# Products that add on in their own banks: three edits around two seven-product stages, key heads in pairs, and small cuts at two norms

## The chip, the cores and the metric

One core of one Trainium2 chip runs the whole program. A core has TensorE (PE in the profile; PEld is its weight load), VectorE (DVE), ScalarE (ACT), GpSimd (POOL), SyncE (SP, which here issues transfers) and 16 DMA engines. Matmul results land in PSUM, eight banks of 128 partitions by 512 fp32 values; everything else is in SBUF. The metric is the device time of one execution in microseconds, as the median of three runs; one execution is also profiled.

## The reference

A two-layer backbone over 256 latent tokens and 256 context tokens, width 1024. Every sub-layer is modulated by a conditioning vector (shift, scale, gate from `ada_w`) and followed by a residual norm:

```python
for i in range(DEPTH):                       # DEPTH = 2
    ml = _modulation(c, ada_w[i], ada_b[i]); mc = _modulation(c_ctx[None, :], ada_w[i], ada_b[i])
    hl = _modulate(x, ml[0], ml[1]); hc = _modulate(xc, mc[0], mc[1])
    # layer 0: mLSTM mixer; layer 1: multi-head latent attention (MLA), 8 heads
    x = _layer_norm(ALPHA * x + ml[2] * yl, ln_g[i, 0], ln_b[i, 0])
    f = _conv_ffn(_modulate(x, ml[3], ml[4]), ffn_w_in[i], ffn_conv_w[i], ffn_conv_b[i], ffn_w_out[i])
    x = _layer_norm(ALPHA * x + ml[5] * f, ln_g[i, 1], ln_b[i, 1])
    # the same for the context tokens xc, in layer 0 only
```

In the mLSTM, `v = x_m @ w_v` (2048 by 2048). In the feed-forward part, `(silu(conv(gate)) * up) @ w_out` (2816 by 1024). In MLA, context and latent tokens give a compressed row `ckv` (256) and a rotary key (64) through `w_dkv`, a norm, and keys and values of the heads through `w_ukv`; queries go through `w_dq` (384) and two further matrices.

## The kernel before, in words

**Precision.** Every fp32 operand is split in two parts, hi (rounded) and lo (the rest), and every product is three matmuls that add up in one bank: hi·hi, hi·lo, lo·hi (`mm3`, L381–L385). A split of a tile is one ScalarE copy for hi and one VectorE subtraction for lo (`split`, L387–L389).

**Weights.** `Stream` (L235–L352) reads the weights in one fixed order: a transfer into a raw tile, a ScalarE copy for hi (L323), a VectorE subtraction for lo (L326). Three split tiles are alive at a time (tile w), further ones are made as early ones are used up, up to eight ahead; some tiles of later use have a wide pool of their own (wu). Loads are issued by SyncE (L281).

**Order.** The program is traced through a scheduler which places each instruction in its engine's queue by dependencies and its own estimate of time, with `keep_in_program_order` (`pin`) for those that must stay where they are written. Background work, such as norms, is a generator that gives up control at each `yield`; `tick(n)` runs n steps of it between matmul groups and `drain` finishes it. `self.ps` takes the next of eight banks in a ring and waits until its last reader is done.

**The two seven-product stages.** `w_v` (L787–L849, banks named tok) computes a 2 by 2 block product with seven block products in place of eight, as sums of operands (S1 to S4) and of results. The results p6, p1, p7, p5 (two banks each, so all eight) come first. ScalarE copies p1 out of its banks, VectorE adds p6 to the copy (u2, later u4), p7 to that (u3), and forms p5 − u3 and p5 − u4; the last three products (weights v21, vt4, v22) then run into three fresh pairs of banks, and VectorE adds them to p1's copy, u3 and u4. It does so twice (two column halves). `w_fout0` (L1365–L1500, banks named y) does the same for the first layer's second feed-forward matrix, in the weight order yt2, y11, yt3, yt1 (six rounds), then y21, y22, yt4 (six each). There each result is also multiplied by the gate (L1454, L1464), added to the scaled residual row (L1455, L1465), and its norm statistics taken (L1457, L1466). `residual()` does this for p1's copy, u4, u3 and the finished fourth block while y21 and y22 run; `add()` does it for the last three products. The context half is normalised (L1507–L1514), transposed (tile zT, L1199), modulated (zm, L1206 and L1208) and split (hc, L1211 and L1212) while yt4 runs; the latent half (hl) follows under the key heads.

**Layer 1's front.** `mla_ctx` makes the context's dkv rows, their norm and transposes (`dkv_T`, L1572–L1581, tile ckT). `ukn(g)` (L1583) makes the keys of eight heads, two in a bank, each head split right after its own matmuls; `uv` (L1598) the values. Then follow `ln_T` of the latent half (L1192), dkv on hl, dq (eight steps over k), `dkv_T` for the latent rows, `ukn(1)` and the queries. `ln_x` (L1218) multiplies the rows by ln_g and ln_b (tiles gr and br, L1227 and L1228) for a later residual.

**Norms.** `ln_rows` (L1131–L1174) normalises a 128-row tile in two halves, VectorE on the first 512 columns (L1172) and ScalarE on the rest (L1173). Where the caller gives the second row tile three banks (`fine`), the first row tile is normalised by ScalarE alone (L1170). `ffn_in` (L1292) of the last layer, with `both`, has for its first pair of tiles (p = 0) a plain mm3 of 256 columns; for the others one matmul of 512 columns covers hi·hi and hi·lo side by side and a second of 256 adds lo·hi, and a copy and an add join the halves. `ada_split` (L454–L460) splits the conditioning matrix's tiles (adas) ahead of the first matmuls (adar, L474).

Of the kernel before, what the change touches and what calls it, by code (L numbers as in the profile page):

```python
# [354 lines left out]
class K:  # L355
# [25 lines left out]
    def mm3(self, out, w, x, start, stop):  # L381
        mm = self.nc.tensor.matmul
        mm(out, w[0], x[0], start=start, stop=False)  # L383
        mm(out, w[0], x[1], start=False, stop=False)  # L384
        mm(out, w[1], x[0], start=False, stop=stop)  # L385
# [68 lines left out]
    def ada_split(self, g):  # L454
        r = []
        for w in self.adaw.pop(g):
            hi, lo = [self.pool.tile([128, 1024], F32R, tag="u", name="adas", bufs=NU) for _ in range(2)]
            self.split(hi, lo, w)
            r.append((hi, lo))
        return r  # L460
# [326 lines left out]
    def w_v(self):  # L787


        nc, st, A = self.nc, self.st, self.xA  # L790
        self.vd = self.dr.tile([H0, 4, 128, 512], F32, name="vd")

        def prod(ps, a, w, h, j):
            for b in range(2):
                ts = slice(b * 128, (b + 1) * 128)
                cs = slice(h * 512, (h + 1) * 512)
                self.mm3(ps[b], (a[:, 0, ts], a[:, 1, ts]), (w[0][:, cs], w[1][:, cs]), j == 0, j == 7)
# [6 lines left out]
        for p in range(2):  # L804
# [9 lines left out]
            u1, u3, u4 = [], [], []  # L814
            for b in range(2):
                u = self.s2("u1")
                nc.scalar.copy(u, p1[b])
                u1.append(u)
                u = self.s2("u2")
                nc.vector.tensor_tensor(u, p6[b], u1[b], op=ALU.add)  # L820
                u4.append(u)
            for b in range(2):
                u = self.s2("u3")
                nc.vector.tensor_tensor(u, p7[b], u4[b], op=ALU.add)
                u3.append(u)
# [14 lines left out]
            for b in range(2):  # L840
                nc.vector.tensor_tensor(u1[b], p2[b], u1[b], op=ALU.add)
                put(2 * p, b, u1[b])
            for b in range(2):
                nc.vector.tensor_tensor(u3[b], p4[b], u3[b], op=ALU.add)
                put(2 * p, 2 + b, u3[b])
            for b in range(2):
                nc.vector.tensor_tensor(u4[b], p3[b], u4[b], op=ALU.add)
                put(2 * p + 1, b, u4[b])
# [282 lines left out]
    def ln_rows(self, pss, xres, gate, fin=None):  # L1131
# [3 lines left out]
        for t in range(2):  # L1135
# [33 lines left out]
            if fine and t == 0:  # L1169
                nc.scalar.activation(z[:, 0:512], z[:, 0:512], AF.Identity, bias=nm, scale=rs)  # L1170
            else:
                nc.vector.tensor_scalar(z[:, 0:512], z[:, 0:512], mv[:, 0:1], rs, op0=ALU.subtract, op1=ALU.mult)  # L1172
            nc.scalar.activation(z[:, 512:1024], z[:, 512:1024], AF.Identity, bias=nm, scale=rs)  # L1173
# [118 lines left out]
    def ffn_in(self, l, hT, n, nt, pre=(), both=None):  # L1292
# [6 lines left out]
        for p in range(NF):  # L1299
            pss = []  # L1300
            for j in range(2):
# [5 lines left out]
                else:  # L1307
# [13 lines left out]
                    if both is not None and p > 0:  # L1321
# [43 lines left out]
    def w_fout0(self, x1d, mid):  # L1365
# [25 lines left out]
        def prod(ps, x, w, i, bs=(0, 1)):  # L1391
            for h in range(2 if i < 5 else 1):
                j = 2 * i + h
                a = A[x, j]
                for b in bs:
                    ts = slice(b * 128, (b + 1) * 128)
                    cs = slice(h * 512, (h + 1) * 512)
                    self.mm3(ps[b], (a[:, 0, ts], a[:, 1, ts]), (w[0][:, cs], w[1][:, cs]), j == 0, j == 10)
# [6 lines left out]
        n = 0  # L1405
        for i in range(6):
            for name, ps, x in (("yt2", p6, "S2"), ("y11", p1, "1"), ("yt3", p7, "S3"), ("yt1", p5, "S1")):
# [21 lines left out]
                n += 1  # L1429
        stats = [self.tiny(12, "st").rearrange("p (a b) -> p a b", b=6) for _ in range(4)]  # L1430
        u1, u3, u4, vv = [], [], [], []
        for b in range(2):
            u = self.s2("u1")
            nc.scalar.copy(u, p1[b])
            u1.append(u)
            u = self.s2("u2")
            nc.vector.tensor_tensor(u, p6[b], u1[b], op=ALU.add)
            u4.append(u)
        for b in range(2):
            u = self.s2("u3")  # L1440
            nc.vector.tensor_tensor(u, p7[b], u4[b], op=ALU.add)
            u3.append(u)
        for b in range(2):
            v = self.s2("v")
            nc.vector.tensor_tensor(v, p5[b], u3[b], op=ALU.subtract)
            nc.vector.tensor_tensor(u4[b], p5[b], u4[b], op=ALU.subtract)
            vv.append(v)

        def residual():

            for us, g, c in ((u1, 0, lo), (u4, 0, hi), (u3, 1, lo), (vv, 1, hi)):
                for b in range(2):
# [7 lines left out]
        def add(g, c, ps):  # L1460
            for b in range(2):
# [522 lines left out]
```

## Time and profile before

| what | value |
|---|---|
| median of 3 runs | 1387.09 us (1386.12 to 1387.57) |
| the profiled execution | 1386.22 us |
| its span, first to last instruction | 1384.1 us |
| outside the span | 2.1 us |
| busy: TensorE, VectorE, ScalarE | 1354.0, 1090.0, 713.1 us |
| mean granted TensorE clock | 0.996 |

The stages named in the text lie here on the time line of the profiled execution: start-up to about 62 us, `w_v` from 207 to 360, `w_fout0` from about 930 to 1044, layer 1's front from there to about 1115, the norm behind the attention output at 1184 to 1190, and the last feed-forward stage to the end. A group's row gives line, engine, operation, tiles as output and inputs, shape and type, a count, and then total busy time and the mean in ns; behind a bar stands the engine's idle time ahead of the group with what ended it. A row of the time line starts with the start and the length in us. A row of waits names the waiting engine and tile, the releasing one, and the total, the count and the longest.

### The profile page before, as it was taken

What the parts mean: (1) busy time and instruction counts of PE and PEld (TensorE: products, weight loads), DVE (VectorE), ACT (ScalarE), POOL (GpSimd) and SP (SyncE); (2) the same over time, 40 slices, a digit from 0 to 9 for tenths busy, and PEclk for the clock granted to TensorE, in tenths of its full rate; (3) what the DMA queues carried; (4) which work ended last, traced back from release to release, by engine and by line L of the source; (5) the groups of instructions that cost most, each with busy time, mean ns of one, the idle gap of its engine ahead of it and who ended that gap; (6) DMA issues with size and microseconds to landing.
All of it is one profiled execution on the core that took longest, in us unless ns stands there. A gap on an engine that the chain in (4) does not pass through costs nothing.

```text
span 1384.1 us, 18592 instructions
## 1 busy us (share of the span) xinstructions
PE 1354.0 (98%) x6567; PEld 1123.2 (81%) x6567; DVE 1090.0 (79%) x1768; ACT 713.1 (52%) x1221; POOL 121.6 (9%) x215
## 2 busy tenths in 40 slices
PE   7999999999999999999999999999999999999997
PEld 3788888888788888878898888888777888888886
DVE  6598857687688697779799878668898789788873
ACT  6585534435444555364643434334637567466660
POOL 0033000011011011120002000000001001000100
PEclk9999999999999999999999999999999999999999
DMA  9689847789666364766747877646987425256750
GB/s 338 227 293 316 290 156 247 239 286 302 214 200 204 105 232 132 250 193 228 241 147 239 300 230 234 212 145 229 312 231 226 137 99 202 109 185 185 252 202 31
DMA packets 97900, 297.58 MB, mean 215 GB/s; under 512 B 12136, under 2 KB 24808, under 8 KB 97808
## 3 DMA queue, kind: packets, MB, share of 16 engines
q1 hardware_dynamic: 68672, 218.52, 47.5%
q0 software_dynamic: 17472, 57.57, 13.3%
q10 hardware_dynamic: 11664, 20.32, 4.1%
q8 instruction: 51, 0.84, 0.2%
q14 instruction: 41, 0.34, 0.1%
HBM read 262.90 MB, written 33.46 MB: 214 GB/s over the span
## 4 chain that ended last, share of the span: by engine, by line
PE 91%; DVE 5%; ACT 2%; issue 1%; DMA 0%; SPq 0%; DVEq 0%; ACTq 0%
PE fin L1320 9%; PE fin L383 6%; PE fin L384 6%; PE fin L385 6%; PE tok L383 6%; PE tok L384 6%; PE tok L385 6%; PE y L384 5%; PE y L385 5%; PE y L383 5%; PE qk L383 4%; PE qk L385 4%; PE qk L384 4%; PE up L383 2%; PE up L385 2%; PE up L384 2%
## 5 line engine op out<-in xcount | busy, mean ns | idle before, releaser
L326 DVE TENSOR_TENSOR w<-raw,w 128x1024 fp32r<-128x1024 f32 (+3 forms) x290 | 348.1, 1203 | 141.3 <-ACT w L323 140.3
L323 ACT CAST w<-raw 128x1024 fp32r<-128x1024 f32 (+3 forms) x290 | 300.4, 1037 | 306.2 <-PE tok L385 88.6
L512 DVE SCALAR_TENSOR_TENSOR junk<-ar,bc 128x1024 f32<-128x1024 f32 x128 | 156.0, 1218 | 4.9 <-ACT bc L554 2.1
L384 PE MATMUL fin<-h,w 128*128 128x512 f32 (+1 forms) x376 | 141.2, 376 | 0.0
L385 PE MATMUL fin<-h,w 128*128 128x512 f32 (+1 forms) x376 | 140.9, 375 | 0.0
L383 PE MATMUL fin<-h,w 128*128 128x512 f32 (+1 forms) x376 | 140.8, 376 | 0.1
L1320 PE MATMUL fin<-h,w 128*128 128x256 f32 (+1 forms) x640 | 113.0, 339 | 0.0
L1320 PEld LDWEIGHTS fin<-h,w 128*128 128x128 f32 x640 | 98.2, 189 | 14.7
L383 PE MATMUL qk<-xc,w 128*128 128x512 f32 x256 | 100.7, 393 | 0.0
L385 PE MATMUL qk<-xc,w 128*128 128x512 f32 x256 | 99.9, 390 | 0.0
L384 PE MATMUL qk<-xc,w 128*128 128x512 f32 x256 | 99.8, 390 | 0.0
L384 PEld LDWEIGHTS fin<-h,w 128*128 128x128 f32 x376 | 70.8, 188 | 12.9 <-DVE h L1212 0.2
L385 PEld LDWEIGHTS fin<-h,w 128*128 128x128 f32 x376 | 70.8, 188 | 12.9
L383 PEld LDWEIGHTS fin<-h,w 128*128 128x128 f32 x376 | 70.5, 188 | 13.1 <-ACT h L1211 0.3
L383 PEld LDWEIGHTS qk<-xc,w 128*128 128x128 f32 x256 | 48.1, 188 | 10.0 <-issue 0.4
L385 PEld LDWEIGHTS qk<-xc,w 128*128 128x128 f32 x256 | 48.1, 188 | 9.9
L384 PEld LDWEIGHTS qk<-xc,w 128*128 128x128 f32 x256 | 48.1, 188 | 9.7
L383 PE MATMUL up<-hT,w 128*128 128x512 f32 x128 | 50.5, 394 | 0.5 <-ACT hT L388 0.5
L384 PE MATMUL up<-hT,w 128*128 128x512 f32 x128 | 50.1, 392 | 0.5 <-DVE hT L389 0.5
L385 PE MATMUL up<-hT,w 128*128 128x512 f32 x128 | 50.1, 391 | 0.3 <-DVE w L389 0.3
L383 PE MATMUL tok<-w,hT 128*128 128x512 f32 x128 | 49.8, 389 | 0.0
L384 PE MATMUL tok<-w,hT 128*128 128x512 f32 x128 | 49.8, 389 | 0.0
(463 smaller groups left out, 3151.2 us busy)
## 6 DMA issues: line engine op xcount, KB each, us to landing
raw<-in_ws SPq DMA_DIRECT2D x287, 512.0 KB, 4.3
ar<-in_adaT SPq DMA_DIRECT2D x80, 512.0 KB, 4.6
adaw<-in_ada_w SPq DMA_DIRECT2D x32, 256.0 KB, 6.7
t2d<-raw ACTq DMA_DIRECT2D x13, 512.0 KB, 4.9
raw<-t2d SPq DMA_DIRECT2D x13, 512.0 KB, 6.3
raw<-in_ws POOLq DMA_DIRECT2D x13, 512.0 KB, 8.0
zr<-fd ACTq DMA_DIRECT2D x33, 128.0 KB, 3.9
xmd<-xr POOLq DMA_DIRECT2D x16, 256.0 KB, 5.0
```

Source lines behind the costliest of these rows:

```text
L323: k.nc.scalar.copy(h[:, :cols], src)
L326: k.nc.vector.tensor_sub(l[:, :cols], src, h[:, :cols])
L383: mm(out, w[0], x[0], start=start, stop=False)
L384: mm(out, w[0], x[1], start=False, stop=False)
L385: mm(out, w[1], x[0], start=False, stop=stop)
L512: nc.vector.scalar_tensor_tensor(o, w, 1.0, self.bc[j], op0=ALU.mult, op1=ALU.mult, accum_out=col[:, k, j:j + 1])
L1320: nc.tensor.matmul(o, a, b, start=k == 0 and i == 0, stop=k == 7 and i == 1)
```

## The change

Six edits. (1) `mm3` gets `on`: with it the first matmul adds to what is in the bank. In both seven-product stages u2 = p6 + p1's copy, as before, but p7 + u2 and p5 − u2 are written back into the banks of p7 and p5, and the last three products add on in the banks of p1, p7 and p5. In `w_v` ScalarE then copies the six finished banks out. In `w_fout0` the copies of p1 are pinned right behind p1's last product, `residual()` is gone, `add` scales the residual itself, and `last` does the fourth block. (2) The last tile of `ada_split(0)` is split in two halves. (3) `ln_rows` with `fine`, second row tile: VectorE takes columns 0–255 and 256–767, ScalarE the last 256. (4) `ffn_in` with `both`: p = 1 also runs as mm3 of 256 columns. (5) `ukn` splits a pair of heads after the second head. (6) `dkv_T(rows, 2)` runs behind the seventh step of dq.

```diff
-    def mm3(self, out, w, x, start, stop):
+    def mm3(self, out, w, x, start, stop, on=False):
...
-        mm(out, w[0], x[0], start=start, stop=False)
+        mm(out, w[0], x[0], start=start, stop=False, skip_group_check=on)
...
     def ada_split(self, g):
+            n = 512 if g == 0 and w is ws[-1] else 1024
+            for i in range(0, 1024, n):
+                self.split(hi[:, i:i + n], lo[:, i:i + n], w[:, i:i + n])
...
     def w_v(self):
-            u1, u3, u4 = [], [], []
+            u2 = []
             for b in range(2):
                 u = self.s2("u1")
                 nc.scalar.copy(u, p1[b])
-                nc.vector.tensor_tensor(u, p6[b], u1[b], op=ALU.add)
-            for b in range(2):
-                nc.vector.tensor_tensor(u, p7[b], u4[b], op=ALU.add)
+                u2.append(u)
+            for b in range(2):
+                nc.vector.tensor_tensor(u2[b], p6[b], u2[b], op=ALU.add)
+            for b in range(2):
+                nc.vector.tensor_tensor(p7[b], p7[b], u2[b], op=ALU.add)
             for b in range(2):
                 v = self.s2("v")
-                nc.vector.tensor_tensor(v, p5[b], u3[b], op=ALU.subtract)
-                nc.vector.tensor_tensor(u4[b], p5[b], u4[b], op=ALU.subtract)
+                nc.scalar.copy(v, p7[b])
+                nc.vector.tensor_tensor(v, p5[b], v, op=ALU.subtract)
+                nc.vector.tensor_tensor(p5[b], p5[b], u2[b], op=ALU.subtract)
                 put(2 * p + 1, 2 + b, v)
-            p2, p4, p3 = pair("tok"), pair("tok"), pair("tok")
             for i in range(4):
-                for name, ps, x in (("v21", p2, 2), ("vt4", p4, 3), ("v22", p3, "S4")):
+                for name, ps, x in (("v21", p1, 2), ("vt4", p7, 3), ("v22", p5, "S4")):
...
-                        prod(ps, A[x, 2 * i + h], w, h, 2 * i + h)
+                        prod(ps, A[x, 2 * i + h], w, h, 2 * i + h, True)
...
-            for b in range(2):
-                nc.vector.tensor_tensor(u1[b], p2[b], u1[b], op=ALU.add)
-                put(2 * p, b, u1[b])
...
+            for q, ps in ((0, p1), (2, p7), (1, p5)):
+                for b in range(2):
+                    v = self.s2("v")
+                    nc.scalar.copy(v, ps[b])
+                    put(2 * p + q % 2, q // 2 * 2 + b, v)
...
     def ln_rows(self, pss, xres, gate, fin=None):
+            cuts = (0,) if fine and t == 0 else (0, 256, 768) if fine else (0, 512)
+            for a, b in zip(cuts, cuts[1:]):
+                nc.vector.tensor_scalar(z[:, a:b], z[:, a:b], mv[:, 0:1], rs, op0=ALU.subtract, op1=ALU.mult)
+            for a, b in ((0, 512), (512, 1024)) if len(cuts) == 1 else ((cuts[-1], 1024),):
+                nc.scalar.activation(z[:, a:b], z[:, a:b], AF.Identity, bias=nm, scale=rs)
...
-                        if both is None or p == 0:
+                        if both is None or p < 2:
...
     def w_fout0(self, x1d, mid):
+                if (name, i) == ("y11", 5):
+                    for b in range(2):
+                        u = self.s2("u1")
+                        pin(nc.scalar.copy(u, p1[b]))
+                        u2.append(u)
...
+        for b in range(2):
+            nc.vector.tensor_tensor(u2[b], p6[b], u2[b], op=ALU.add)
+        for b in range(2):
+            nc.vector.tensor_tensor(p7[b], p7[b], u2[b], op=ALU.add)
         for b in range(2):
             v = self.s2("v")
-            nc.vector.tensor_tensor(v, p5[b], u3[b], op=ALU.subtract)
-            nc.vector.tensor_tensor(u4[b], p5[b], u4[b], op=ALU.subtract)
+            nc.scalar.copy(v, p7[b])
+            nc.vector.tensor_tensor(v, p5[b], v, op=ALU.subtract)
+            nc.vector.tensor_tensor(p5[b], p5[b], u2[b], op=ALU.subtract)
             vv.append(v)
-        def residual():
-            for us, g, c in ((u1, 0, lo), (u4, 0, hi), (u3, 1, lo), (vv, 1, hi)):
-                for b in range(2):
-                    zz = z[2 * g + b]
-                    nc.vector.tensor_tensor(us[b], us[b], gate[g][:, c], op=ALU.mult)
-                    nc.vector.scalar_tensor_tensor(zz[:, c], zz[:, c], ALPHA, us[b], op0=ALU.mult, op1=ALU.add)
-                    if us is vv:
-                        nc.vector.bn_stats(stats[2 * g + b][:, 1], zz[:, c])
-                    yield
+        def add(g, c, ps, bs=(0, 1)):
+            for b in bs:
...
-                nc.vector.tensor_tensor(zz, zz, t, op=ALU.add)
+                nc.vector.scalar_tensor_tensor(zz, zz, ALPHA, t, op0=ALU.mult, op1=ALU.add)
...
+        def last():
+            for b in range(2):
+                add(1, hi, vv, (b,))
+                yield
-            prod(ps, "2", w, i)
-            if i == 1:
-                self.bg.append(residual())
+            prod(p1, "2", w, i, on=True)
...
-        add(0, lo, ps)
-        ps = pair()
+        add(0, lo, p1)
+        self.bg.append(last())
         for i in range(6):
             w = st.use(("y22", 0, i))
-            prod(ps, "S4", w, i)
+            prod(p5, "S4", w, i, on=True)
...
-            prod(ps, "3", w, i)
+            prod(p7, "3", w, i, on=True)
...
     def ukn(self, g):
-            u = self.kn[h]
-            self.split(u[:, 0, cs], u[:, 1, cs], ps[:, hs])
+            if h % 2:
+                for j in range(2):
+                    u = self.kn[h - 1 + j]
+                    self.split(u[:, 0, cs], u[:, 1, cs], ps[:, j * 256:(j + 1) * 256])
...
     def mla(self, hl):
+                if k == 6:
+                    self.dkv_T(rows, 2)
...
-        self.dkv_T(rows, 2)
```

More of the change, by code (lines that the diff above doesn't have):

```diff
@@ L455, in ada_split @@
         r = []
-        for w in self.adaw.pop(g):
+        ws = self.adaw.pop(g)
+        for w in ws:
             hi, lo = [self.pool.tile([128, 1024], F32R, tag="u", name="adas", bufs=NU) for _ in range(2)]
-            self.split(hi, lo, w)
+            n = 512 if g == 0 and w is ws[-1] else 1024
+            for i in range(0, 1024, n):
+                self.split(hi[:, i:i + n], lo[:, i:i + n], w[:, i:i + n])
             r.append((hi, lo))
@@ L791, in w_v, with prod @@
         self.vd = self.dr.tile([H0, 4, 128, 512], F32, name="vd")
-        def prod(ps, a, w, h, j):
+        def prod(ps, a, w, h, j, on=False):
             for b in range(2):
@@ L796, in prod @@
                 cs = slice(h * 512, (h + 1) * 512)
-                self.mm3(ps[b], (a[:, 0, ts], a[:, 1, ts]), (w[0][:, cs], w[1][:, cs]), j == 0, j == 7)
+                self.mm3(ps[b], (a[:, 0, ts], a[:, 1, ts]), (w[0][:, cs], w[1][:, cs]), j == 0 and not on, j == 7, on)
         def pair(name):
@@ L1320, in ffn_in @@
                             nc.tensor.matmul(o, a, b, start=k == 0 and i == 0, stop=k == 7 and i == 1)
-                    if both is not None and p > 0:
+                    if both is not None and p > 1:
                         t = self.s2("fs")
@@ L1389, in operand, with prod @@
                     A[x, j] = u[:, :, h * 256:(h + 1) * 256]
[L1391 removed]
+        def prod(ps, x, w, i, bs=(0, 1), on=False):
             for h in range(2 if i < 5 else 1):
@@ L1397, in prod @@
                     cs = slice(h * 512, (h + 1) * 512)
-                    self.mm3(ps[b], (a[:, 0, ts], a[:, 1, ts]), (w[0][:, cs], w[1][:, cs]), j == 0, j == 10)
+                    self.mm3(ps[b], (a[:, 0, ts], a[:, 1, ts]), (w[0][:, cs], w[1][:, cs]), j == 0 and not on, j == 10, on)
         def pair():
@@ L1405, in w_fout0 @@
         n = 0
+        u2 = []
         for i in range(6):
@@ L1483, in w_fout0 @@
         self.drain()
-        add(0, hi, ps)
+        add(0, hi, p5)
         self.bg = [mid(0, z[0:2], stats[0:2])]
         self.step(self.bg)
-        ps = pair()
         for i in range(6 - YTAIL):
             w = st.use(("yt4", 0, i))
-            prod(ps, "3", w, i)
+            prod(p7, "3", w, i, on=True)
             self.tick(2)
@@ L1496, in w_fout0 @@
             for i, w in ws:
-                prod(ps, "3", w, i, (b,))
+                prod(p7, "3", w, i, (b,), True)
         st.unhold("yt4")
         self.fa = self.fd = None
-        self.bg = [mid(1, z[2:4], stats[2:4], lambda: add(1, lo, ps))]
+        self.bg = [mid(1, z[2:4], stats[2:4], lambda: add(1, lo, p7))]
     def z_norm(self, zs, stats):
```

33 lines of the change are left out of this document (3 added, 30 removed).

## The prediction

> **What bounds the kernel now.** I read the page's busy shares, its clock line and its chain first, to see which engine sets the end.
>
> ```profile
> span 1384.1 us, 18592 instructions
> ...
> PE 1354.0 (98%) x6567; PEld 1123.2 (81%) x6567; DVE 1090.0 (79%) x1768; ACT 713.1 (52%) x1221; POOL 121.6 (9%) x215
> ...
> PE 91%; DVE 5%; ACT 2%; issue 1%; DMA 0%; SPq 0%; DVEq 0%; ACTq 0%
> ```
>
> TensorE is busy 98% of the span and is 91% of the chain. An edit that adds no matmul can win only where TensorE stands still, and there is little of that: 1384.1 − 1354.0 = 30 us, start-up included. So the second view is TensorE's waits, each with the instruction that ended it.
>
> ```profile
> PE adar L474 <- ACT adas L388: 6.8, 1, 6.8
> PE y L384 <- DVE w L326: 3.2, 3, 1.4
> ...
> PE zT L1199 <- DVE z L1172: 1.8, 1, 1.8
> PE y L383 <- ACT u L1434: 1.5, 1, 1.5
> PE dkv L383 <- ACT hl L1211: 1.5, 1, 1.5
> ...
> PE kn L383 <- ACT ckT L1576: 0.7, 1, 0.7
> ```
>
> The edits lie at these waits: the u copy (L1434) and the late weights (L326) in the second seven-product stage, the hl casts behind the key heads, ckT ahead of the second key heads, and z (L1172) ahead of the last feed-forward stage. No row shows a wait in the first seven-product stage (tile tok). Third, the windows around these places, with the granted clock in the third column from the right:
>
> ```profile
> 998.00:1010.00 12.00, 9.58 (x40) 7.00 (x39) 11.43 (x16) 8.48 (x12) 0.00 (x0) 1.00 0.75 269
> 1023.00:1042.00 19.00, 17.61 (x76) 13.92 (x75) 19.00 (x28) 8.61 (x10) 4.05 (x6) 1.00 0.97 253
> 1043.00:1047.00 4.00, 3.17 (x21) 2.28 (x20) 2.74 (x7) 3.33 (x8) 0.86 (x2) 1.00 1.03 231
> ...
> 1074.00:1084.00 10.00, 8.40 (x42) 7.34 (x41) 9.12 (x21) 6.16 (x16) 0.25 (x1) 0.83 0.00 0
> ...
> 1184.00:1193.00 9.00, 6.83 (x41) 5.73 (x40) 6.61 (x19) 6.83 (x16) 0.00 (x0) 0.81 0.03 10
> ```
>
> Columns are PE, PEld, DVE, ACT, POOL busy, clock, DMA share, GB/s. VectorE is full in 1023–1042 (19.00 of 19 us): that stage is bound by VectorE wherever TensorE stands. Two windows have a clock below 1: a mean of 0.83 over 10 us is 10 × 0.17 × 2 = 3.4 us at half clock, and 0.81 over 9 us is again 3.4 us. Half clock for 3.4 us costs at most 1.7 us.
>
> **The change part by part.** All times below are on before's own time line. Two durations recur:
>
> ```profile
> 1023.68 0.39 PE L385 MATMUL y<-w,fz 128*128 128x512 f32 x1
> 1023.91 0.61 PE L383 MATMUL y<-w,fz 128*128 128x512 f32 x2
> 1025.88 0.50 PE L384 MATMUL y<-w,fz 128*128 128x512 f32 x1 [1.35 <-DVE w L326]
> ```
>
> A matmul on 512 columns starts 0.23 us after the one before it; the row's 0.39 includes its pipeline.
>
> ```profile
> 1006.58 0.68 DVE L1445 TENSOR_TENSOR v<-y,u 128x512 f32<-128x512 f32 x1
> 1007.18 0.68 DVE L1446 TENSOR_TENSOR u<-y,u 128x512 f32<-128x512 f32 x1
> 1007.77 2.35 DVE L326 TENSOR_TENSOR w<-raw,w 128x1024 fp32r<-128x1024 f32 x2
> ```
>
> A VectorE operation on 512 columns holds its engine 0.60 us (1006.58 to 1007.18), a weight split (L326) 1.14 us or so (2.35 for two, less the tail).
>
> *First ada tile in halves.* The last 1024-column tile becomes two halves.
>
> ```profile
> 10.64 1.05 ACT L388 CAST adas<-adaw 128x1024 fp32r<-128x1024 f32 x1 [0.37 <-DMA adaw<-in_ada_w]
> ...
> 11.73 1.23 DVE L389 TENSOR_TENSOR adas<-adaw,adas 128x1024 fp32r<-128x1024 f32 x1 [0.19 <-ACT adas L388]
> ...
> 13.01 0.86 PE L474 MATMUL adar<-adas,condr 128*4 128x512 f32 x3 [0.33 <-DVE adas L389]
> ...
> 13.90 0.58 ACT L477 COPY adarow<-adar 4x512 f32<-4x512 f32 x1 [0.92 <-PE adar L474]
> ```
>
> The cast of the tile runs 10.64–11.69, its split to 12.96, then three matmuls, then the copy at 13.90. In halves the first split starts half a cast earlier and one or two matmuls are left behind the second: the split ends about 12.65 and the copy starts about 13.1. **−0.8** (0 to −0.8: none, if the transfers that follow set the start-up instead).
>
> *First seven-product stage.* Six VectorE adds per pass become six ScalarE copies and two more copies stand between p7 and its subtraction. The accumulation is off every wait row above, and ScalarE is half idle. **0** (±0.3 for the two p7 copies that VectorE now waits for in each of two passes).
>
> An unknown is a VectorE result written into a bank, of which the trace has no row. The nearest rows are a result from a bank into SBUF, 0.68 us (the L1446 row above), and, further off, a 256-column operation and the 1024-column split of 1.23 (11.73 above):
>
> ```profile
> L1212 DVE TENSOR_TENSOR hc<-zm,hc 128x256 fp32r<-128x256 f32 x8 | 3.0, 422 | 2.6 <-ACT hc L1211 2.6
> ```
>
> I take 0.68, the same shape, and 0.42 and 1.23 us as ends: with four such results in the stage below this is −1.0 to +2.2 us.
>
> *Second seven-product stage.* What y21 waited for before:
>
> ```profile
> 1000.75 0.62 ACT L1386 CAST fz<-zr 128x512 fp32r<-128x512 f32 x1 [0.53 <-DMA zr<-fd]
> 1001.27 0.58 ACT L1434 COPY u<-y 128x512 f32<-128x512 f32 x1
> ...
> 1001.90 0.50 PE L383 MATMUL y<-w,fz 128*128 128x512 f32 x1 [1.53 <-ACT u L1434]
> ```
>
> All eight banks were taken, so y21's new pair waited for the copy of p1. Now the copies are issued right after p1's last matmul, 12 matmuls (2.7 us) earlier, and y21 adds on in p1: the 1.5 us wait goes. Next late is y21's first weight, whose cast stands behind the two copies and whose split stands behind three VectorE sums: done 1001.3, a stall of 0.75. The next split is behind the v and p5 sums: 0.9, as the 0.9 before (part of the 3.2 row). Then VectorE does less: sums 8 as before; gating, scaling and statistics fall from 36 operations (residual 18, add 18) to 24. Twelve operations × 0.60 = 7.2 us less in a stretch where VectorE was full and the weights came late; so the 1.35 us stall at 1025.88 goes (I place the later splits 0.35 to 0.85 us ahead of need). What is late last is the norm behind y22:
>
> ```profile
> 1046.78 0.42 PE L383 MATMUL dkv<-w,hc 128*128 128x320 f32 x1 [0.32 <-ACT hc L1211]
> ```
>
> y22 ends 3.5 us sooner, but the norm chain has one weight split more in it (10.2 us, from 1031.2, against 8.4): the cast of hc ends and dkv starts at about 1043.9. **−2.9**. Its cover: of 1.5 + 2.1 + the small gaps, some 6.6 us of lost time in 1000–1047, about 3.8 stay.
>
> *Key heads in pairs.* Now the order of TensorE is all key heads, 12 value matmuls, 16 transposes, 12 value matmuls, dkv on hl; before these were mixed. The work, from the groups in 1047–1090:
>
> ```profile
> L383 PE MATMUL dkv<-w,hl 128*128 128x320 f32 x16 | 5.7, 356 | 1.5 <-ACT hl L1211 1.5
> ...
> L383 PE MATMUL kn<-ckT,wu 128*128 128x256 f32 x16 | 4.7, 294 | 0.0
> ...
> L383 PE MATMUL v<-wu,ckT 128*128 128x512 f32 x8 | 3.2, 403 | 0.0
> ...
> L1199 PE MATMUL zT<-ident,z 128*128 128x128 f32 x16 | 2.5, 276 | 0.0
> ```
>
> Each mm3 has three such lines (L383 to L385): 48 key, 24 value, 48 dkv matmuls and 16 transposes. Their spacing, and the ends of the stretch:
>
> ```profile
> 1061.47 0.28 PE L383 MATMUL kn<-ckT,wu 128*128 128x256 f32 x1
> 1061.58 0.28 PE L384 MATMUL kn<-ckT,wu 128*128 128x256 f32 x1
> ...
> 1071.97 0.60 PE L1199 MATMUL zT<-ident,z 128*128 128x128 f32 x4
> ...
> 1087.30 0.31 PE L385 MATMUL dkv<-w,hl 128*128 128x320 f32 x1
> 1087.45 0.51 PE L383 MATMUL dq<-w,hl 128*128 128x384 f32 x2
> ```
>
> Key matmuls start 0.115 us apart, dkv's 0.15, transposes (0.60 − 0.28) / 3 = 0.11: 48 × 0.115 + 24 × 0.227 + 16 × 0.11 + 48 × 0.15 = 5.5 + 5.4 + 1.8 + 7.2 = 19.9 us. From 1061.47 to 1087.45 it took 26.0: 6.1 lost. In the new order I place the last weight splits ahead of need, four transposes 0.5 late (they wait for a bank), the hl cast 0.95 late and its low part 0.5 late: about 2 us lost, without a half-clock window. **−4.0**, of which 1.7 is the window. What hides the key heads' splits, now in two's, is the value matmuls between.
>
> *What is behind it.* VectorE's six operations with gr and br move in front of dq's first low weight:
>
> ```profile
> 1075.55 1.89 DVE L1227 TENSOR_TENSOR z<-z,gr 128x512 f32<-128x512 f32 x3
> ```
>
> Six × 0.60 = 3.6 us, and v's splits; dq's first split is then done at about 1082.3: **+1.35** (0 if they fall in the wait for hl). With dkv's transposes moved behind dq's seventh step the 0.7 wait at ckT goes, some transposes' own gaps with it (−1.3), and the query stage waits for its own evacuation, 0.5: **−0.8**.
>
> *Norm before the last feed-forward stage.* VectorE normalises columns 0–255 first:
>
> ```profile
> 1187.09 0.54 DVE L1172 TENSOR_SCALAR z<-z,mv,rs 128x512 f32<-128x512 f32 x1
> ```
>
> A pass of half the columns takes about half of 0.54 (0.24 to 0.27 less), so the transposes start 0.24 us sooner, and the four first matmuls fill a later gap: **−0.5** (0 to −1.8, the whole wait). Its half clock stays.
>
> *Sixteen more matmuls.* Per step a 512-column and a 256-column matmul (0.23 + 0.115) become three of 256 (0.35): **+0.2** for sixteen steps, and a copy and an add go from engines with time to spare.
>
> **The sum.** −0.8 + 0 − 2.9 − 4.0 + 1.35 − 0.8 − 0.5 + 0.2 = −7.4. The profiled run took 1386.22 us, 2.1 more than its span, so 1378.8 for a run like it. It lies 0.9 under the median of the runs shown (1387.09), which would become **1379.7**.
>
> **The rivals.**
>
> (a) *The half clock stays* behind the key heads, or comes once more at another gap. For it: 0.83 in 1074–1084 came with 8.40 of 10 us busy, so no long idle is needed, and I still forecast 2 us lost there. Against it: less is lost in one piece. It costs 1.7: 1381.4. The Trainium skill, "TensorE: Matmul & The Clock Gate", Part 1, has the clock fall after an idle window of about 3.4 us on a free-running grid. By that rule neither place should have fallen to half, since no wait row above is over 1.8 us behind start-up; the trace disagrees, and so I don't take short gaps as safe.
>
> (b) *Only the second seven-product stage and the start-up win*, because the splits of heads and values still stand in front of hl's casts and the six moved operations in front of dq. For it: VectorE was 9.12 of 10 us busy in 1074–1084, ScalarE 6.16. Against it: the key heads' part before was mostly late weights, and these now come during key heads. 1387.1 − 0.8 − 2.9 = 1383.4.
>
> (c) *Slower.* Key heads now fill the front of the stretch, and each pair has four splits that alternate between ScalarE and VectorE. Where VectorE also has the value weights' splits in hand, each head's low part stands behind one of them: 8 × 1.14 = 9.1 us, and the transposes' evacuation and hl's casts are queued behind all of it on both engines; with the half-clock window of 1.7 again, 10.8: 1390.5. It decides where over 10.2 us are lost in this way (7.4 + 2.8), so from seven of the eight heads on. For it: VectorE was 9.12 of 10 us busy in 1074–1084. Against it: weight splits come as the stream's tiles come free, and I place only four behind the first key head. Beside it the Trainium skill, "PSUM — Partial Sum Buffer", section "PSUM bank collisions raise a hardware error", says that two engines may not touch one bank at once and that software must order them: adding on in a bank that ScalarE and VectorE still use can only be by waiting. The 1.5 us row at y shows such a wait before the change; no run shows yet what it is behind it.
>
> (d) *It doesn't do what it says*: the copies of p1 stand behind casts on ScalarE (two weight casts of 1 us), the sums in the banks take longer than 0.68, and y21 waits as before. Nothing then comes sooner for the key heads, and start-up and the sixteen matmuls alone are left: 1387.1 − 0.8 + 0.2 = 1386.5.
>
> **How the numbers follow.** Forecast 0.48 (1377 to 1381), (a) 0.20, (b) 0.16, (d) 0.09, (c) 0.07. The range reaches from 1375.5 (late weights vanish altogether in the second stage, 2 us, and the norm's whole wait, 1.3) to 1385.0, which takes in (a) and (b). A measurement of this kernel tells about 0.2%, 2.8 us: (b) lies 3.7 under, so one time in five within it. Faster 0.48 + 0.20 + 0.13 = 0.81; same 0.03 + 0.09 = 0.12; slower 0.07.
>
> **What would show it.** In the changed profile: dkv on hc starts 2.9 + 0.8 us sooner and no row "y ← ACT u" is left; two stalls of about 0.8 us at y21's first weights; dq starts 7.6 us sooner, with clock 1.00 over that window; a new wait of dq on a weight split of 1.3 us; no wait at ckT; the first adarow copy at 13.1. Wrong would make it: the half clock still there (a), rows "dkv ← ACT hl" over 2 us (b, c), or y21 waiting for a copy (d).

## The result, and the profile after

The changed kernel takes 1379.68 us (median; 1379.17 to 1380.86), the kernel before 1387.09 (1386.12 to 1387.57): ratio 0.9949, 95% interval 0.9934 to 0.9964. The profiled execution went from 1386.22 to 1379.68 us, by 6.5. The page of the changed kernel, the lines that answer to the first ones of the prediction:

```profile
span 1377.9 us, 18614 instructions
...
PE 1349.8 (98%) x6583; PEld 1121.5 (81%) x6583; DVE 1074.9 (78%) x1744; ACT 719.8 (52%) x1238; POOL 121.4 (9%) x215
...
PE 89%; DVE 5%; ACT 2%; DMA 2%; issue 1%; SPq 0%; ACTq 0%; DVEq 0%
```

TensorE still sets the end. VectorE does 15 us less (1090.0 to 1074.9), ScalarE 7 us more. TensorE's waits, to be read against the same view of before in the prediction:

```profile
PE adar L478 <- ACT adas L389: 7.0, 1, 7.0
PE y L385 <- DVE w L326: 2.9, 3, 1.1
PE zT L1197 <- DVE z L1169: 1.7, 1, 1.7
...
PE dq L385 <- DVE w L326: 1.0, 1, 1.0
PE y L385 <- DVE wu L326: 0.8, 1, 0.8
PE dkv L384 <- ACT hc L1209: 0.7, 1, 0.7
PE dkv L384 <- ACT hl L1209: 0.7, 1, 0.7
```

Gone are y behind the u copy (1.5) and kn behind ckT (0.7); dkv behind the hl cast is 0.7 where it was 1.5. New are dq behind a weight split (1.0) and y behind a wu split (0.8), the latter at 688 us, in a stage that no edit touches.

Single executions differ by more than most edits are worth, so the parts are read from stretches of TensorE's time line between fixed matmuls, in all fourteen traces. Each column is the time from one start to the next: the program's start to the first tok matmul; the last matmul of mout's first weights (tiles y, hn) to the last one of yt1; from there to dkv on hc; to dkv on hl; to dq; to the last qr; and the last aout matmul to the end.

| kernel | to tok | hn to yt1 | yt1 to hc | hc to hl | hl to dq | dq to qr | aout to end |
|---|---|---|---|---|---|---|---|
| before | 120.77 | 316.47 | 46.79 | 31.63 | 9.04 | 20.65 | 199.60 |
| after | 120.06 | 317.89 | 44.21 | 29.11 | 7.86 | 21.08 | 198.48 |
| e1 halved tile alone | 122.72 | 317.58 | 47.53 | 31.62 | 9.03 | 20.65 | 198.80 |
| e2 no halved tile | 120.94 | 317.39 | 43.92 | 29.10 | 7.87 | 21.09 | 199.36 |
| e3 w_fout0 as before | 121.47 | 317.28 | 47.75 | 29.12 | 7.87 | 21.09 | 199.48 |
| e4 no pairs | 120.97 | 316.87 | 43.55 | 31.62 | 7.49 | 19.93 | 199.37 |
| e5 pairs alone | 121.34 | 316.56 | 46.80 | 29.12 | 7.87 | 22.55 | 199.46 |
| e6 dkv_T not moved | 121.29 | 317.25 | 43.26 | 29.14 | 7.86 | 22.59 | 199.37 |
| e7 ln_x behind the heads | 121.48 | 316.83 | 43.93 | 29.12 | 7.42 | 19.81 | 207.21 |
| e8 sums spread | 120.81 | 317.31 | 44.06 | 29.12 | 7.86 | 21.08 | 199.35 |
| e9 w_v as before | 120.47 | 316.76 | 43.57 | 29.12 | 7.87 | 21.05 | 198.48 |
| e10 p = 1 as before | 120.93 | 316.86 | 43.96 | 29.10 | 7.86 | 21.07 | 199.37 |
| e11 ln_x behind dq | 121.02 | 316.95 | 43.80 | 29.10 | 7.43 | 19.82 | 199.38 |
| e12 twelve operations more | 120.93 | 316.87 | 47.96 | 29.11 | 7.86 | 21.08 | 199.46 |

The second column covers code that no kernel here changes up to its last microseconds, and it spreads over 1.4 us; "to tok" spreads over 2.7 us (see e1 and e2), and "yt1 to hc" over 1 us within one form. In the other four, kernels with the same code there repeat to some 0.1 us, but for the steps that the granted clock makes (below).

### The profile page after: what moved, and what is told of

Read it like the earlier page. It is cut to its first block, busy times and chain, and to the rows that moved or that the text cites. A ratio compares the mean times of both kernels' runs of the same rounds, so it can differ in the third digit from the quotient of the medians.

```text
span 1377.9 us, 18614 instructions
## 1 busy us (share of the span) xinstructions
PE 1349.8 (98%) x6583; PEld 1121.5 (81%) x6583; DVE 1074.9 (78%) x1744; ACT 719.8 (52%) x1238; POOL 121.4 (9%) x215
## 4 chain that ended last, share of the span: by engine, by line
PE 89%; DVE 5%; ACT 2%; DMA 2%; issue 1%; SPq 0%; ACTq 0%; DVEq 0%
PE fin L1318 8%; PE fin L385 6%; PE fin L384 6%; PE fin L386 6%; PE tok L384 6%; PE tok L385 6%; PE tok L386 6%; PE y L385 5%; PE y L386 5%; PE y L384 5%; PE qk L384 4%; PE qk L386 4%; PE qk L385 4%; PE up L384 2%; PE up L386 2%; PE up L385 2%
## 5 line engine op out<-in xcount | busy, mean ns | idle before, releaser
L385 PEld LDWEIGHTS fin<-h,w 128*128 128x128 f32 x376 | 70.8, 188 | 13.1 <-DVE h L1210 0.2
```

The source lines that it names most:

```text
L385: mm(out, w[0], x[1], start=False, stop=False, skip_group_check=on)
```

## The experiments

**e1 and e2: the halved conditioning tile.** e2 is the changed kernel without it, as in this diff; e1 is the kernel before with it:

```diff
...
-            n = 512 if g == 0 and w is ws[-1] else 1024
-            for i in range(0, 1024, n):
-                self.split(hi[:, i:i + n], lo[:, i:i + n], w[:, i:i + n])
+            self.split(hi, lo, w)
```

> The kernel before with the halved conditioning tile alone. Theory A (the gain of the start-up is lost again where a weight's transfer sets the pace): the first adarow copy at 13.1 to 13.2, TensorE 0.7 ahead of before up to 680 us, then a wait of about 1 us at the mixer's last output weights (tile wu, near 688) and no lead behind it: 1387.0, within 0.3 of before. Theory B (the wait near 688 in the changed kernel was chance of that one run): no such wait, 0.7 ahead to the end: 1386.4.

> The changed kernel without the halved tile. Theory A: TensorE is 0.7 later up to 680, waits only about 0.2 near 688, and stands from there where the changed kernel stands: 1379.7. Theory B: 0.7 later to the end: 1380.4.

e1: 1385.89 us beside 1386.27 for before, ratio 0.9999 (0.9990 to 1.0008). e2: 1379.94, ratio 0.9955 (0.9939 to 0.9970), where the changed kernel has 0.9949. The tile makes no difference that can be measured in the medians, as theory A said, but not for its reason: no lead is lost at 688 us. The wait there, start to start beyond the matmuls' own spacing, is 1.03 in e1, e2 and the changed kernel alike, though none but the last had a lead, and over all fourteen traces it lies anywhere from 0.20 (before) to 1.03. It is a weight that came late, as the changed kernel's ScalarE shows:

```profile
686.93 1.05 ACT L323 CAST wu<-raw 128x1024 fp32r<-128x1024 f32 x1 [1.20 <-DMA raw<-in_ws]
```

The first tok matmul comes at 121.0 us on average in the three traces without the halves (before, e2, e5) and at 121.1 in the eleven with them. TensorE's rows of before (two), e2 and the changed kernel, in this order:

```profile
10.12 2.56 PE L474 MATMUL adar<-adas,condr 128*4 128x512 f32 x8 [0.20 <-DVE adas L389]
...
13.01 0.86 PE L474 MATMUL adar<-adas,condr 128*4 128x512 f32 x3 [0.33 <-DVE adas L389]
```

```profile
8.21 5.82 PE L475 MATMUL adar<-adas,condr 128*4 128x512 f32 x15 [0.67 <-DVE adas L390]
```

```profile
8.27 4.89 PE L478 MATMUL adar<-adas,condr 128*4 128x512 f32 x15 [0.67 <-DVE adas L390]
```

What differs is the clock. The trace's record of the granted clock opens, at full, at 10.6 us in the changed kernel, 11.1 in before, 12.7 in e2 and 15.5 in e1. Ahead of that moment these matmuls start 0.43 us apart where nothing holds them, from it on 0.23. (A window ahead of it reads 1.00, because nothing is recorded there.) The first adarow copy follows, at 13.19, 13.90, 14.06 and 15.88 us, and from it to the first tok matmul all fourteen traces take 106.8 to 106.9 us: what is won or lost here is kept. Where the full clock comes early, TensorE catches up and waits for the last split (13.01 in before); only there can halves win something, and how much no pair of traces with the same clock shows. Where it comes late, TensorE still has its own queue of matmuls and is itself the last.

**e3: the second seven-product stage as before,** all else changed.

```diff
-            prod(p1, "2", w, i, on=True)
+            prod(ps, "2", w, i)
+            if i == 1:
+                self.bg.append(residual())
```

> The changed kernel with the second seven-product stage as before (three fresh pairs of banks, residual in the background). Theory A (terms add up): the wait of y on the u copy is back with 1.5 us, the stall of about 1.5 near 1024 too, dkv on hc starts 2.6 us later than in the changed kernel, and the time is 1382.3. Rival: what is lost there is taken up by the key heads behind it (they wait for the norm on VectorE anyway), then dq starts at the same time as in the changed kernel and the time is 1379.7; or the half clock comes back and it is 1384.

1383.34 us, ratio to before 0.9981 (0.9971 to 0.9990): 3.7 over the changed kernel. Theory A holds in kind, with more than its 2.6. In TensorE's waits from yt1 to dkv on hc the u copy is back:

```profile
PE y L384 <- ACT u L1432: 2.7, 1, 2.7
PE y L385 <- DVE w L326: 2.1, 2, 1.3
PE zT L1197 <- DVE z L1511: 0.5, 1, 0.5
PE dkv L384 <- ACT hc L1209: 0.3, 1, 0.3
```

The stretch is 47.8 us, and the stretches behind it, up to the last qr, are those of the changed kernel to 0.03 us: nothing takes the loss up there.

**e4 and e5: the pairs of key heads.** e4 is the changed kernel without them, e5 the kernel before with them alone.

```diff
-            if h % 2:
-                for j in range(2):
-                    u = self.kn[h - 1 + j]
-                    self.split(u[:, 0, cs], u[:, 1, cs], ps[:, j * 256:(j + 1) * 256])
+            u = self.kn[h]
+            self.split(u[:, 0, cs], u[:, 1, cs], ps[:, hs])
```

> The changed kernel with each key head split right behind its own matmuls. Theory A (the new order of the key heads wins 3.7 us, 1.7 of it the half clock): dkv on hl waits over 1.4 us for the hl cast, the clock falls to half there, dq starts 3.7 later against dkv on hc than in the changed kernel: 1383.4. Rival (it was the earlier weights out of the stage before, and the clock grid, not the pairs): dq starts within 0.5 of the changed kernel's: 1379.9.

> The kernel before with the key heads split in pairs, and nothing else of the change. From dkv on hc to the last matmul of qr before took 61.3 us, with the half clock in it, the changed kernel 58.1 and the changed kernel without pairs 59.1, both without the half clock. Theory A (pairs win by the order alone, 2.2 us to dq, and lose 1.15 at dq's first weight; the half clock is worth 1.5 more where it falls on the grid): 61.3 − 1.0 − 1.5 = 58.8 for this stretch if the clock stays full, 60.3 if not; time 1384.0 to 1385.6. Theory B (the pairs win nothing without the weights that the stage before frees): the weight splits are late again, 60.8 or more: 1386.5.

e4: 1381.02 us, ratio 0.9961 (0.9949 to 0.9974). To dkv on hl it loses 2.5 us, as theory A said in kind, but the clock did not fall. The same place in before, in e4 and in the changed kernel (clock in the third column from the right):

```profile
1074.00:1088.00 14.00, 12.40 (x69) 11.34 (x68) 12.80 (x25) 7.88 (x20) 2.18 (x4) 0.88 0.20 65
```

```profile
1070.00:1084.00 14.00, 12.39 (x76) 11.05 (x75) 12.98 (x27) 8.70 (x22) 1.63 (x3) 1.00 0.10 37
```

```profile
1070.00:1084.00 14.00, 11.90 (x69) 10.48 (x70) 13.94 (x31) 10.39 (x27) 1.63 (x3) 1.00 0.13 49
```

Before and e4 both waited 1.68 us for the hl cast (start to start, beyond the matmul's own spacing), and only one was slowed: 9.04 against 7.49 us from hl to dq, so 1.55 for the half clock. e4 also has no wait at dq, which the pairs have; from hc to qr the pairs win 59.05 − 58.05 = 1.0 us.

e5: 1385.83, ratio 0.9999 (0.9990 to 1.0009). From hc to qr 59.5 us: neither theory's number. Before took 61.3, or 59.8 without the half clock; the order wins its 2.5 to dkv on hl without the edit ahead of it, so theory B falls, but dq to qr takes 22.55 in place of 20.65, of which 1.1 is the wait at dq that the pairs bring. Alone, the pairs are worth 0.2 us and the chance of not falling to half clock.

**e6: the latent transposes behind dq, as before.**

```diff
-                if k == 6:
-                    self.dkv_T(rows, 2)
+        self.dkv_T(rows, 2)
```

> The changed kernel with the latent rows' transposes behind dq, as before. Theory A: the wait of kn on ckT is back with 0.7 to 0.9, a 0.35 wait at qr goes, and the stretch from dkv on hc to the last qr takes 58.6 to 58.8 where the changed kernel takes 58.1; time 0.6 over the changed kernel, 1380.3. Rival: with dq's first weight late anyway the move is free, and the stretch stays at 58.1.

1381.12 us, ratio 0.9963 (0.9950 to 0.9976). The wait of kn is back:

```profile
PE kn L384 <- ACT ckT L1565: 1.0, 1, 1.0
```

From hc to qr 59.6 us, 1.55 over the changed kernel: theory A in kind, with more than twice its size. Without the pairs the move wins 0.7 (59.77, which is before without the half clock, to 59.05 in e4). Pairs and move are worth more together (1.7) than one by one (0.2 + 0.7).

**e7 and e11: the operations on gr and br elsewhere.** They stand ahead of dq's first split; e7 writes them behind the attention's heads, e11 behind dq.

```diff
-        k.take_late()
         att = k.mla(hl)
         oT = next(att)
+        k.take_late()
+        k.drain()
```

> The changed kernel with the eight operations that multiply by gr and add br (the later residual) written behind the attention's heads instead of ahead of dkv on hl. Theory A (they are what holds back dq's first weight split): the 1.1 us wait of dq goes, and 1.1 us is won to the end: 1378.6. Rival (the split waits for its cast on ScalarE, or the operations cost as much beside the heads): the wait stays, or the heads' own waits grow by the same; 1379.7.

And e11:

```diff
-        k.take_late()
         att = k.mla(hl)
...
+        self.take_late()
         cq = []
```

> The changed kernel with the eight operations on gr and br taken up behind dq: later than in the changed kernel, earlier than behind the heads. Theory A (these operations hold back dq's first weight and hl's last low parts; written behind the heads they came so late that the residual's transfer was late at the norm): dkv on hc to the last qr takes 56.3 to 56.6 us where the changed kernel takes 58.1, no wait of 4 us at the norm behind aout, 1378.2. Rival: they now stand ahead of the rotary operations of the queries, the transposes of qr wait for them by 1 us or more, and the time is 1379.7 again.

e7: 1386.90 us, ratio 1.0006 (0.9997 to 1.0016); e11: 1383.58, 0.9979 (0.9970 to 0.9988). In both the wait of dq is gone, and hc to qr takes 56.3 us in place of 58.05: those operations did hold dq back. Both lose more later. The waits of e7 around the norm behind aout, and of e11 behind qr:

```profile
PE zT L1197 <- ACT z L1171: 4.7, 1, 4.7
PE zT L1197 <- DVE z L1169: 4.1, 1, 4.1
```

```profile
PE qrT L1713 <- DVE qrs L1685: 2.0, 1, 2.0
PE s L384 <- ACT qn L1704: 1.4, 1, 1.4
```

In e7 the rows come late, and behind them in GpSimd's queue the loads that the norm needs, the gate above all. GpSimd and then VectorE show it:

```profile
1160.80 1.07 POOL L1227 DMA_DIRECT2D x2d<-z  x2 [1.50 <-DVE z L1226]
1161.87 1.14 POOL L1267 DMA_DIRECT2D xres<-x2d  x2
...
1165.53 1.08 POOL L1125 DMA_DIRECT2D gate<-gd  x2
```

```profile
1173.97 0.69 DVE L1139 TENSOR_TENSOR z<-y,gate 128x512 f32<-128x512 f32 x1 [4.48 <-DMA gate<-gd]
```

In the changed kernel xres is issued from 1131.4 on and gate from 1138.9. In e11 the eight operations stand ahead of the queries' rotary part (L1521 begins at 1108.19, when the queries' matmuls already run). Behind the queries e11 loses 5.4 us and e7 8.0, against a trace such as e2's; in both a part is half clock that the longer waits brought with them (3.4 us behind qr in e11; 10.2 us at the norm in e7, where most traces have 3.4). The 1.7 us that the operations cost ahead of dq is the cheapest of three places. Theory A of e7 was right on the wait and wrong on the sum; in e11 the rival named the wait that came, though not its size.

**e8: the sums into p7 and p5 spread over y21's steps.**

```diff
-        for b in range(2):
-            nc.vector.tensor_tensor(p7[b], p7[b], u2[b], op=ALU.add)
+        def folds():
+            yield
...
+            for b in range(2):
+                nc.vector.tensor_tensor(p7[b], p7[b], u2[b], op=ALU.add)
+            yield
...
+        self.bg.append(folds())
         for i in range(6):
             w = st.use(("y21", 0, i))
```

> The changed kernel with the sums into p7 and p5 spread over y21's steps instead of being written ahead of them. Theory A (the 0.9 us wait near 1008 is a weight split that stands behind four sums on VectorE): it goes, the 1.2 us wait at y21's first weight stays (three sums are still in front): dkv on hc starts 0.9 sooner against the last yt1 matmul, 1378.8. Rival (the weight is late through its transfer or its cast): both waits stay as they are, 1379.7.

1378.13 us, ratio 0.9947 (0.9932 to 0.9962), the same as the changed kernel. Its waits from yt1 to hc:

```profile
PE y L385 <- DVE w L326: 1.2, 2, 0.9
PE zT L1197 <- DVE z L1511: 0.9, 1, 0.9
PE dkv L384 <- ACT hc L1209: 0.7, 1, 0.7
```

The 0.9 us near 1008 is gone (theory A's cause), and 0.9 has come up behind yt4, where TensorE waits for the norm: 44.06 us from yt1 to hc, where the eight traces of the changed form take 43.3 to 44.2. VectorE does the same work. That the stage ends when this work is through fits, but e8 does not show it; e12 puts it to the test.

**e9 and e10: the first seven-product stage, and the sixteen matmuls, as before.**

```diff
-                for name, ps, x in (("v21", p1, 2), ("vt4", p7, 3), ("v22", p5, "S4")):
+            p2, p4, p3 = pair("tok"), pair("tok"), pair("tok")
...
+                for name, ps, x in (("v21", p2, 2), ("vt4", p4, 3), ("v22", p3, "S4")):
```

and for e10

```diff
-                        if both is None or p < 2:
+                        if both is None or p == 0:
```

> The changed kernel with the first seven-product stage as before (fresh banks for the last three products). Theory A: nothing waited there before and nothing does now; from the first matmul with tile tok to the last (239.4 us in both kernels) nothing changes by more than 0.2 us, and the time is 1379.7. Rival: the two passes' copies of p7 in front of VectorE's subtraction cost 0.3 each, so this one is 0.6 shorter there.

> The changed kernel with the last feed-forward stage's second pair of tiles as before (one 512-column and one 256-column matmul per step). From the last matmul of aout to the end the changed kernel takes 198.5 us with the clock full and 199.4 with the half clock behind that norm, before 198.8 and 199.6. Theory A (sixteen more matmuls cost 0.2, the cut norm wins 0.5): 0.2 shorter than the changed kernel, 198.3 or 199.2. Rival (the copy and the add that the edit saves are worth more than the matmuls cost): 0.2 or more longer, 198.7 or 199.6.

e9 (`w_v` of the kernel before): 1378.96 us, ratio 0.9947 (0.9932 to 0.9961); first to last tok matmul 239.41, and 239.51 in the changed kernel. Accumulating in place is worth nothing there (0.1 us the wrong way). e10: 1380.23, ratio 0.9955 (0.9939 to 0.9972); aout to end 199.37, and 199.36 in e2, which has the sixteen matmuls and the same half clock. They cost nothing that can be seen; both theories are off by 0.2.

**e12: twelve multiplications more on VectorE** beside y21 and y22; their results are used by nothing.

```diff
+        def extra():
+            for n in range(6):
+                g, c = n % 2, (lo, hi)[n // 2 % 2]
+                t = self.s2("zx")
+                nc.vector.tensor_tensor(t, z[2 * g][:, c], gate[g][:, c], op=ALU.mult)
+                nc.vector.tensor_tensor(t, t, gate[g][:, c], op=ALU.mult)
+                yield
...
+            if i == 1:
+                self.bg.append(extra())
```

> The changed kernel with twelve 512-column multiplications on VectorE added beside y21 and y22, in the place where the residual operations stood; their results are used by nothing. From the last yt1 matmul to dkv on hc the stage took 46.8 to 47.8 us in the four runs of the old form and 43.3 to 44.2 in the eight of the new one. Theory A (the stage's end is set by how much VectorE has to do, and the 7.2 us of operations taken off it are the gain): 46 to 47 us, and 1382. Theory B (the gain is the wait for the banks at y21, 1.5 to 2.8 us, and VectorE has room for the rest): 44.0 to 44.5 us, and 1380.

1383.08 us, ratio to before 0.9977 (0.9967 to 0.9987): 3.4 over the changed kernel, with no wait for a copy of p1:

```profile
PE y L385 <- DVE w L326: 3.5, 3, 1.9
PE zT L1197 <- DVE z L1512: 0.5, 1, 0.5
```

VectorE is nearly full again. Its busy time is the third figure, for before, the changed kernel and e12:

```profile
1000.00:1045.00 45.00, 40.68 (x176) 31.91 (x175) 44.77 (x70) 21.98 (x29) 6.96 (x9) 1.00 0.84 234
```

```profile
1000.00:1045.00 45.00, 42.33 (x191) 33.64 (x189) 39.69 (x59) 26.22 (x36) 7.25 (x9) 1.00 0.89 255
```

```profile
1000.00:1045.00 45.00, 41.54 (x172) 32.67 (x171) 43.77 (x66) 22.41 (x29) 5.12 (x6) 0.96 0.84 238
```

From yt1 to hc e12 takes 47.96 us. In it is a half clock that this trace alone has there,

```profile
1022.00:1032.00 10.00, 8.07 (x29) 6.18 (x28) 9.77 (x15) 1.87 (x3) 1.75 (x2) 0.83 0.88 213
```

10 × 0.17 = 1.7 us at most; without it at least 46.3, against 43.8 on average in the eight traces of the changed form. Theory A holds: at least 2.5 of the stage's 3.4 us are VectorE's work. The medians, over ten executions each, say the same: e12 gives back 3.4 us where e3 gives back 3.7.

## Why the prediction was right

The total came out as forecast: 1379.7 forecast, 1379.68 measured, within the range and on the forecast side. That it fits to 0.1 us is luck: the working aimed at the profiled run, 1378.8, and that took 1379.68. The two large terms, which carry the gain, have the mechanism that was written (a part of one, the clock, may be chance) and come within 0.5 us in size; among the small ones errors cancel. The terms, one by one:

- **The halved tile, −0.8: not shown; 0 on average.** The changed kernel's first copy did come at 13.19, where the working has 13.1, and the 0.7 us lasts to tok. But what this step took as fixed, that TensorE has caught up when the last split comes, so that "one or two matmuls are left behind the second", depends on when the full clock is granted (10.6 to 15.5 us here). In e1 and e2 TensorE is still in its own queue of fifteen matmuls.
- **First seven-product stage, 0: right** (+0.1, e9).
- **A VectorE result into a bank: 0.69 us,** 0.68 taken:

```profile
1001.10 0.69 DVE L1439 TENSOR_TENSOR y<-y,u 128x512 f32<-128x512 f32 x1
```

- **Second seven-product stage, −2.9: right in kind; −3.4.** Mean of the four old-form stretches 47.2 (before, e1, e3, e5), of the eight new ones 43.8. The placed stalls were there: 0.75 forecast at y21's first weight, 0.6 to 1.3 measured; 0.9 at the next, 0.9 measured; none near 1025; dkv last behind the hc cast, as written. e12 shows which part carried it: VectorE's twelve operations at least 2.5, so the freed banks 0.9 at most.
- **Key heads in pairs, −4.0 to dq: right in size; −3.7** (31.63 + 9.04 to 29.11 + 7.86). Of the placed waits, 0.5 at zT, 0.95 and 0.5 at hl, the trace has 0.53, 0.81 and 0.62. The half clock in it was priced 1.7 and measured 1.55, but e4 shows that it can stay away with the same wait. Of three traces in the old order two have it, of eleven in the new order none: the pairs may make it rarer, which these traces do not settle. So 1.55 of this term may be luck.
- **Behind it, +1.35 and −0.8: +0.43 measured where +0.55 was forecast.** The cost and the gain were both taken too small, and the two errors cancel. Without the move the pairs cost 1.9 from dq to qr (20.65 to 22.55, e5), 1.1 of it the wait at dq; the moved transposes win back 1.5 beside the pairs (e6).
- **The norm and the sixteen matmuls, −0.5 + 0.2: −0.1 to −0.3.** aout to end falls from 198.80 (e1) to 198.48 (after, e9) with the full clock, and from 199.5 (before, e5) to 199.4 with the half clock. No experiment split the cut norm from the rest of this stretch by itself; e10 leaves it all to the norm. (The working's own spacings, 0.23 + 0.115 against 0.35, give under 0.1 for the sixteen matmuls, not 0.2.) "Its half clock stays" did not hold in the profiled run: the clock there was 1.00, which is worth 0.9 us and, as e2 shows, is not the edit's doing.

The sum of measured terms, 0 + 0.1 − 3.4 − 3.7 + 0.4 − 0.2, is −6.8 us. In the profiled pair itself the spans differ by 6.2: −0.7 to tok, +1.4 from hn to yt1, where weights near 688 and 984 us came late, −2.6 from yt1 to hc, −3.7 to dq, +0.4 to qr and −1.1 behind aout, 0.9 of it the clock. So of the signs that the prediction names, dkv on hc came 1.8 us sooner and not 3.7, and dq 5.5 and not 7.6; the waits named there came or went as written, and so did the full clock behind the key heads.

Of the rivals, (b), little from the second half, has against it e4 to e6: the front of layer 1 keeps 3.3 us, of which 1.55 is the clock. (c), a block by the splits, did not come: the waits for hl's cast and its low part are 0.7 and 0.5 us. (Its condition is also mis-summed: seven heads give 7 × 1.14 + 1.7 = 9.7 us, under the 10.2 that it needs; it takes all eight.) (d) is out by the missing u row. On (a) see the last section.

## What to carry to other kernels

A wait that names a buffer can hide an engine that is full: when a bank was freed and VectorE was given its work back, the time came back though the wait did not (e12), and when one stall in the same stage was smoothed, another of the same length rose behind it (e8). Price such an edit by the work that it takes off the full engine, in the stage where it is full. Work that is "not urgent" has a price wherever it stands: try its places (1.7 us ahead of dq, 5.4 in e11, 8 in e7) before moving it. And where single executions differ by more than an edit, compare stretches between fixed instructions, over several kernels that share the code.

## What the runs showed of the hardware

The slow TensorE clock is not set by how long TensorE idles alone. Behind the key heads the same 1.68 us wait brought 3.4 us of half clock in before and e1 and none in e4. Behind aout, with waits of 0.43 and 1.87 us in identical code, the changed kernel and e9 kept full clock, and eight others did not:

```profile
1178.00:1188.00 10.00, 7.63 (x59) 6.66 (x58) 8.07 (x25) 6.81 (x16) 0.00 (x0) 1.00 0.10 39
```

```profile
1178.00:1188.00 10.00, 8.03 (x51) 7.09 (x51) 8.07 (x25) 6.80 (x16) 0.00 (x0) 0.83 0.09 35
```

The first is the changed kernel, the second e2; to the end the one takes 198.48 us, the other 199.36. The Trainium skill, "TensorE: Matmul & The Clock Gate", Part 1, has a free-running window of 3413 ns and a fall after a whole idle one. The free grid agrees with these traces: every fall comes a whole number of 3413 ns steps behind the first record of full clock (313 in before, 343 in e2), and where the wait lies on this grid differs from run to run. The whole idle window does not agree: in e2 TensorE was busy for 8.0 of the 10 us, with no gap over 1.9.

At one place in the code, how long TensorE was busy in the step that holds the wait goes with the fall. At the norm it was busy for 1.4 us of the 3.4 in e2 (1180.1 to 1183.5), which fell, and for 1.7 in e9 and at least 1.8 in the changed kernel, whose waits lie across two steps; those did not. Behind the key heads it was 1.8 in before (1076.1 to 1079.5), which fell, and 2.0 in e4, which did not. Across places and kernels this is no rule: 1.8 fell and 1.7 did not, and e1 kept the full clock behind a step with 1.5 at the norm. What sets the fall stays open.
